# The input in a second, transposed layout, and its mean square through a product with ones

## The chip, the cores and the metric

The kernel runs on one core of a Trainium2 chip. The metric is the device time of one execution in microseconds; the profile and the trace are of one profiled execution. Engines: PE is TensorE (matmul), PEld its weight loads, DVE is VectorE, ACT is ScalarE, POOL is GpSimd, SP issues most of the DMAs. ACT issues DMAs too.

## The reference, cut to what matters

One layer of an encoder with 256 tokens and a width of 2048, all in float32. Only the first lines bear on the change:

```python
def rms_norm(x, w):
    y = x * lax.rsqrt(jnp.mean(x * x, axis=-1, keepdims=True) + EPS)
    return y * w

h = rms_norm(x, norm_mix_pre)
proj = jnp.einsum('bsd,dc->bsc', h, w_in)          # [256, 10240]
qa, ka, va, qn, kn, vn, gates = jnp.split(proj, split_at, axis=-1)
qa = apply_rope(qa, cos, sin); ka = apply_rope(ka, cos, sin)
...
x = x + rms_norm(y, norm_mix_post)
```

After it come two attentions (differential and neighbourhood), gates, an output projection with its norm and residual, and an MLP of width 8192 with squared ReLU. The factor rsqrt(mean(x²) + eps) is one number per token. It can be applied after the projection, and the kernel does so: it multiplies the rows of cos and sin by it (for qa and ka), or the values on their way out of PSUM.

## The kernel before, in words

Every float32 product is made of parts: a matrix w is split into hi (rounded to float32r by a cast on ACT) and lo = w - hi (a subtraction on DVE), both in `split` (L115 and L116). The activations are split likewise and lie as [128 | hi 256 | lo 256], so that one matmul with hi of the weight (L191, 512 wide) and one with lo (L192, 256 wide) make a product.

`wgroup` computes 512 columns of a projection, transposed, in four PSUM banks of [128 columns, 512]; it goes over the 2048 rows of the weight in four chunks of four row blocks. The pool `mm` holds exactly four such banks. A bank is emptied by `halves`: ACT copies its right half (L254), DVE adds that to the left half (L256). `agroup` is its counterpart for values (L229 to L231). `load` issues one weight chunk of 1 MB from SP into one of three buffers.

The first group is qa with columns QA to QA + 512. The lines around the change:

- The input x comes in four pieces of 512 columns, as [128 tokens, 2, 512], from SP (L144, L149), between the first three chunks of the weight (L146, L98).
- `x_parts(i)` transposes four blocks of x on TensorE (L268, against the identity) into a PSUM bank, and makes hi (L273, ACT, times the gain g_pre) and lo (L274, DVE) of them in hT.
- `x_squares(i)` squares a piece of x on ACT with a sum along the row (L345), so ssx holds sums per token, tokens on partitions.
- `prelude(ch)` is called ahead of chunk ch of the first group: it traces `x_parts` one chunk ahead, and the squares at chunks 2 and 3.
- `postlude` is called in the last chunk, after the products of bank 0 and ahead of its emptying: it issues small inputs, calls `row_scales` and `head_constants`.
- `row_scales` adds up ssx (L300), takes the mean plus eps (L85) to the power -0.5 on POOL (L88; rx is [128 tokens, 2]), and by `along_tokens` makes of it a row of all tokens on all partitions, rxb [128, 256]: a diagonal matrix on DVE (L77), a product with ones on TensorE (L78), a copy on ACT (L79). Then rxs (L303), and cosT and sinT times rxb (L304, L305).

The emptying of a qa or ka bank goes on with `rope_evac`: products with sinT and cosT, a sum, and the split in parts (L385 to L388, L371, L372).

The order of the instructions on each engine is made by a planner at build time, from the order in which they are traced and from its own estimates of their times; `tc.issue_after` adds an order by hand. At run time each engine takes its instructions in that order.

Of the kernel before, what the change touches and what calls it, by code (L numbers as in the profile page):

```python
# [17 lines left out]
P = 128  # L18
D = 2048
# [19 lines left out]
def encoder_layer(ctx: ExitStack, tc: tile.TileContext, a, out):  # L39
# [32 lines left out]
    def along_tokens(r, b, name):  # L72
        """r [P tokens, token tile] as a row of all tokens, on all partitions."""
        ps = bank(f"{name}_p")
        for t in range(2):
            dg = t1k(f"{name}_d{t}")
            nc.vector.tensor_scalar_mul(dg[:, :P], ident, r[:, t : t + 1])  # L77
            nc.tensor.matmul(ps[:, t * P : (t + 1) * P], ones, dg[:, :P], start=True, stop=True)  # L78
        nc.scalar.copy(b, ps[:, :T])  # L79

    def inv_rms(ss, n, name, r=None):
        """(ss / n + eps) ** -0.5, per partition."""
        w = ss.shape[1]
        ms_ = small(w, f"{name}_m")
        nc.vector.tensor_scalar(ms_, ss, 1.0 / n, EPS, op0=ALU.mult, op1=ALU.add)  # L85
        if r is None:
            r = small(w, f"{name}_r")
        nc.gpsimd.tensor_tensor(r, ms_, expo[:, :w], op=ALU.pow)  # L88
        return r

# [1 line left out]
    last_load = [None]  # L92

    def load(src, k0, nk, c0, cw, name):
        """Rows k0*128.. of a weight: [P, nk, cw]."""
        raw = wp.tile([P, nk, cw], F32, tag="raw", name=f"{name}_w")
        view = src[k0 * P : (k0 + nk) * P, c0 : c0 + cw].rearrange("(k p) c -> p k c", p=P)
        last_load[0] = nc.sync.dma_start(raw, view).ins  # L98
        return raw

    def split(raw, name, pieces=2, after=()):
        """Two float32r parts whose sum is raw. after[s] are instructions that go ahead of piece s."""
        _, nk, cw = raw.shape
        hi = wp.tile([P, nk, cw], F32R, tag="hi", name=f"{name}_h")
        lo = wp.tile([P, nk, cw], F32R, tag="lo", name=f"{name}_l")
        for s in range(pieces):
            part = (
                (slice(None), slice(s * nk // pieces, (s + 1) * nk // pieces))
                if nk > 1
                else (slice(None), slice(None), slice(s * cw // pieces, (s + 1) * cw // pieces))  # L110
            )
            with ExitStack() as order:
                for ins in after[s] if after else ():
                    order.enter_context(tc.issue_after(ins))
                nc.scalar.copy(hi[part], raw[part])  # L115
                nc.vector.tensor_sub(lo[part], raw[part], hi[part].bitcast(F32))  # L116
        return hi, lo
# [3 lines left out]

# [1 line left out]
    g_pre = const.tile([P, KD], F32, name="g_pre")  # L123
# [6 lines left out]
    nc.gpsimd.memset(ones, 1.0)  # L130
    x = a["x"]
    xv = x.rearrange("(t p) c -> p t c", p=P)
    xp = []
    first = []
    for i in range(4):
        xt = page([P, 2, 512], F32, f"x_{i}")
        xi = xv[:, :, i * 512 : (i + 1) * 512]
        xp.append(xt)
        if i == 0:
            raw = wp.tile([P, 4, 512], F32, tag="raw", name="first0_w")  # L140
            view = a["w_in"][: 4 * P, QA : QA + 512].rearrange("(k p) c -> p k c", p=P)
            for h in range(2):
                cs = slice(h * 256, (h + 1) * 256)
                nc.sync.dma_start(xt[:, :, cs], xi[:, :, cs])  # L144
                for k in range(h * 2, h * 2 + 2):
                    nc.sync.dma_start(raw[:, k], view[:, k])  # L146
            first.append(raw)
        else:
            nc.sync.dma_start(xt, xi)  # L149
            if i < 3:  # L150
                first.append(load(a["w_in"], i * 4, 4, QA, 512, f"first{i}"))
    g_mlp = const.tile([P, KD], F32, name="g_mlp")
# [19 lines left out]
    def advance(n):  # L172
        """Trace the next n stages of the attention heads that wait for their turn, and one chore."""
        if chores:
            with tc.issue_after(last_load[0]):
                chores.pop(0)()
        for _ in range(n):
            if pending:
                g = pending.pop(0)
                if next(g, None):  # L180
                    pending.append(g)

    def wgroup(src, c0, act, nk, evac, name, first=(), hook=None, mid=None, after={}, k_first=False, inner=None):
        """out^T of 512 columns: weights stationary. act(k) is [P, hi 256 | lo 256]."""
        ps = [bank(f"{name}_p{b}", True) for b in range(4)]
# [34 lines left out]
    def agroup(src, c0, stat, nk, evac, name, tail=1, between=None):  # L220
        """out of 512 columns: activations stationary. stat(k, t) is (hi, lo) of [P, 128].
        The last ``tail`` chunks go token tile by token tile; between(i) may trace instructions
        ahead of the i-th of the second tile's products there and returns the last of them."""
        ps = [bank(f"{name}_p{t}", True) for t in range(2)]
# [26 lines left out]
    def halves(ps, name):  # L251
        """The sum of the two halves of a bank, in SBUF."""
        r = t1k(f"{name}_r")
# [4 lines left out]

# [1 line left out]
    hT = [page([P, 2, 512], F32R, f"hT{i}") for i in range(8)]  # L260

    def x_parts(i):
        """The transpose of four tiles of x times the gain, in two parts [P, hi | lo]."""
        acts = []
        for k in range(i * 4, i * 4 + 4):
            pt = bank(f"hT_t{k}")
            for t in range(2):
                nc.tensor.transpose(  # L268
                    pt[:, t * P : (t + 1) * P], xp[i][:, t, (k % 4) * P : (k % 4 + 1) * P], ident
                )  # L270
            d = hT[k // 2][:, k % 2]
            g = g_pre[:, k : k + 1]
            acts.append(nc.scalar.activation(d[:, :T], pt[:, :T], AF.Copy, scale=g).ins)  # L273
            nc.vector.scalar_tensor_tensor(  # L274
                d[:, T:], pt[:, :T], g, d[:, :T].bitcast(F32), op0=ALU.mult, op1=ALU.subtract
            )

        return acts
# [16 lines left out]

    ssx = const.tile([P, 8], F32, name="ssx")

    def row_scales():
        sx = small(2, "sx")
        nc.vector.tensor_reduce(sx, ssx.rearrange("p (t h) -> p t h", h=4), axis=AX.X, op=ALU.add)  # L300
        inv_rms(sx, D, "rx", rx)
        along_tokens(rx, rxb, "rxb")
        nc.vector.tensor_scalar_mul(rxs, rx, SCALE)  # L303
# [15 lines left out]

    # Position bias: row (h, i) of rpbp holds the bias of row offset i - 3 at column offsets  # L320
    # -63..63. Each is written 64 times at a pitch of 127 and read at a pitch of 126.
    def skew_write(h):
# [18 lines left out]

    def x_squares(i):
        for t in range(2):
            j = junk512("jx0").rearrange("p a b -> p (a b)")
            nc.scalar.activation(  # L345
                j, xp[i][:, t], AF.Square, accum_out=ssx[:, t * 4 + i : t * 4 + i + 1]
            )

    def postlude():
# [15 lines left out]

# [1 line left out]
    oT = {}  # L367
# [6 lines left out]
    def product3(ps, stat, s_at, mov, m_at, start, stop):  # L374
        """ps (+)= stat^T @ mov, each given in two parts."""
        for i, (sp, mp) in enumerate(((0, 0), (0, 1), (1, 0))):
# [42 lines left out]
    def p_transposed(p, name):  # L419
        """[P queries, (t, keys)] -> [P keys, (key tile, queries)]"""  # L420
        pt = bank(f"{name}_pt")
# [171 lines left out]

# [1 line left out]
    mT = []  # L595
# [26 lines left out]

# [1 line left out]
    def mstat(k, t):  # L624
# [9 lines left out]
    for t in range(2):  # L634
        for h in range(2):
            nc.sync.dma_start(
                x2[t * 2 + h], x[t * P : (t + 1) * P, h * 1024 : (h + 1) * 1024]
            )
# [77 lines left out]

# [1 line left out]
    def first_up_inner(k):  # L718
# [103 lines left out]
def _host_arrays(inputs):  # L822
    f = {k: np.ascontiguousarray(v) for k, v in inputs.items()}
    arr = {
        "x": f["x"][0],
        "w_in": f["w_in"][0],
        "w_branch_a": f["w_branch_a"][0],
# [12 lines left out]
        "lam_k2": f["lam_k2"],  # L840
        # row offsets -3..3 are the ones that four rows reach
        "rpbp": np.pad(f["na_rpb"][0][:, 4:11], ((0, 0), (0, 0), (48, 48))),
# [30 lines left out]
```

## Time and profile before

| what | value |
|---|---|
| median of 3 runs | 1397.62 us (1397.48 to 1398.73) |
| span of the profiled execution | 1394.5 us |
| median of the runs less that span | 3.1 us |
| TensorE busy | 1374.6 us, 99% of the span |
| DVE, ACT, POOL busy | 835.8, 668.7, 7.9 us |
| first transpose, first product of qa | 3.95, 9.41 us |
| first product of ka | 36.58 us |

The profiled execution is known by its span, from the first to the last instruction. All times within it count from the span's start. A row of the trace in order of time reads: start, duration, engine, line, operation, written tile <- read tiles, shapes, count, and in brackets how long the engine had been idle and what ended that. Rows that follow each other on an engine are merged (x2, x4), their duration then being the stretch from the first start to the last end.

### The profile page before, as it was taken

The numbers are of one execution on the slowest core, as the hardware profiler recorded it, in microseconds if no ns is written. First come the engines' busy times: TensorE is split into PE (matmuls) and PEld (weight loads), VectorE is DVE, ScalarE is ACT, GpSimd is POOL, SyncE is SP. The second block draws the span as 40 slices with busy tenths as digits, with TensorE's granted clock in tenths as the row PEclk, the third lists the DMA queues.
The fourth block names the chain that finished last, engine by engine and source line by source line (L and its number), as shares of the span: only waits on it lengthen the run. The fifth ranks groups of instructions, "written<-read, shape, count | busy, mean of one in ns | idle before, by whom it ended". The sixth has DMA issues, their size and how long they took to land.

```text
span 1394.5 us, 17896 instructions
## 1 busy us (share of the span) xinstructions
PE 1374.6 (99%) x7240; PEld 1177.8 (84%) x7240; DVE 835.8 (60%) x1155; ACT 668.7 (48%) x1023; POOL 7.9 (1%) x19
## 2 busy tenths in 40 slices
PE   7999999999999999999899999999999999999997
PEld 6888888888888888888788888888888888888886
DVE  6868866676656565654755555555575554444445
ACT  7554554545444445543744444444464543334332
POOL 0000000000000000000000000000000000000000
PEclk9999999999999999999999999999999999999999
DMA  9674755564555555675455565656555556555551
GB/s 317 202 214 154 202 177 173 171 191 155 165 205 182 203 181 183 203 279 184 149 182 181 182 193 170 211 170 200 189 196 185 203 186 227 195 187 205 181 199 73
DMA packets 117490, 265.16 MB, mean 190 GB/s; under 512 B 15008, under 2 KB 16288, under 8 KB 109216
## 3 DMA queue, kind: packets, MB, share of 16 engines
q1 hardware_dynamic: 117264, 264.03, 57.3%
q8 instruction: 56, 0.92, 0.3%
q14 instruction: 26, 0.21, 0.0%
q10 hardware_dynamic: 144, 0.01, 0.0%
HBM read 261.92 MB, written 3.92 MB: 191 GB/s over the span
## 4 chain that ended last, share of the span: by engine, by line
PE 98%; DVE 1%; DMA 0%; ACT 0%; SPq 0%; issue 0%; DVEq 0%; POOLq 0%; POOL 0%; ACTq 0%
PE u_p L191 17%; PE u_p L192 9%; PE acc L779 8%; PE acc L778 8%; PE acc L777 8%; PE gb_p L191 4%; PE ga_p L191 4%; PE qa_p L191 2%; PE gb_p L192 2%; PE ga_p L192 2%; PE ka_p L191 2%; PE qn_p L191 2%; PE bb_p L191 2%; PE ba_p L191 2%; PE kn_p L191 2%; PE y_p L229 2%
## 5 line engine op out<-in xcount | busy, mean ns | idle before, releaser
L191 PE MATMUL u_p<-h2T,u_h 128*128 128x512 f32 x1024 | 359.9, 398 | 0.5 <-DVE r_m L85 0.5
L192 PE MATMUL u_p<-h2T,u_l 128*128 128x256 f32 x1024 | 284.3, 280 | 0.0
L116 DVE TENSOR_TENSOR d_l<-d_w,d_h 128x1024 fp32r<-128x1024 f32 x128 | 151.1, 1221 | 164.2 <-ACT d_h L115 163.7
L116 DVE TENSOR_TENSOR u_l<-u_w,u_h 128x1024 fp32r<-128x1024 f32 x128 | 151.1, 1222 | 146.0 <-ACT u_h L115 144.7
L191 PEld LDWEIGHTS u_p<-h2T,u_h 128*128 128x128 f32 x1024 | 192.0, 189 | 45.5 <-DVE r_m L85 0.9
L115 ACT CAST d_h<-d_w 128x1024 fp32r<-128x1024 f32 x128 | 128.3, 1052 | 191.1 <-PE acc L779 187.5
L778 PE MATMUL acc<-d_l,uh 128*128 128x512 f32 x512 | 199.0, 389 | 0.0
L779 PE MATMUL acc<-d_h,ul 128*128 128x512 f32 x512 | 198.9, 389 | 0.0
L777 PE MATMUL acc<-d_h,uh 128*128 128x512 f32 x512 | 198.2, 389 | 0.0
L192 PEld LDWEIGHTS u_p<-h2T,u_l 128*128 128x128 f32 x1024 | 193.8, 189 | 1.3
L115 ACT CAST u_h<-u_w 128x1024 fp32r<-128x1024 f32 x128 | 128.0, 1049 | 123.9 <-PE u_p L191 62.5
L778 PEld LDWEIGHTS acc<-d_l,uh 128*128 128x128 f32 x512 | 96.1, 188 | 20.1
L777 PEld LDWEIGHTS acc<-d_h,uh 128*128 128x128 f32 x512 | 96.1, 188 | 20.0
L779 PEld LDWEIGHTS acc<-d_h,ul 128*128 128x128 f32 x512 | 96.1, 188 | 19.8
L191 PE MATMUL gb_p<-hT,gb_h 128*128 128x512 f32 x256 | 90.4, 398 | 0.0
L191 PE MATMUL ga_p<-hT,ga_h 128*128 128x512 f32 x256 | 90.0, 397 | 0.0
L192 PE MATMUL gb_p<-hT,gb_l 128*128 128x256 f32 x256 | 71.4, 281 | 0.0
L192 PE MATMUL ga_p<-hT,ga_l 128*128 128x256 f32 x256 | 70.3, 280 | 0.0
L191 PEld LDWEIGHTS gb_p<-hT,gb_h 128*128 128x128 f32 x256 | 47.9, 188 | 11.5
L116 DVE TENSOR_TENSOR gb_l<-gb_w,gb_h 128x1024 fp32r<-128x1024 f32 x32 | 37.8, 1221 | 31.1 <-ACT gb_h L115 31.1
L191 PEld LDWEIGHTS ga_p<-hT,ga_h 128*128 128x128 f32 x256 | 47.4, 188 | 10.5
L116 DVE TENSOR_TENSOR y_l<-y_w,y_h 128x1024 fp32r<-128x1024 f32 x32 | 37.9, 1222 | 27.8 <-ACT y_h L115 27.8
(213 smaller groups left out, 2348.1 us busy)
## 6 DMA issues: line engine op xcount, KB each, us to landing
u_w<-in_w_up SPq DMA_DIRECT2D x64, 1024.0 KB, 5.4
d_w<-in_w_down SPq DMA_DIRECT2D x64, 1024.0 KB, 4.9
ga_w<-in_w_in SPq DMA_DIRECT2D x16, 1024.0 KB, 5.2
gb_w<-in_w_in SPq DMA_DIRECT2D x16, 1024.0 KB, 5.2
y_w<-in_w_out SPq DMA_DIRECT2D x16, 1024.0 KB, 5.1
ka_w<-in_w_in SPq DMA_DIRECT2D x8, 1024.0 KB, 6.1
va_w<-in_w_in SPq DMA_DIRECT2D x8, 1024.0 KB, 5.2
qn_w<-in_w_in SPq DMA_DIRECT2D x8, 1024.0 KB, 5.1
```

The costliest lines, as they stand in the source:

```text
L115: nc.scalar.copy(hi[part], raw[part])
L116: nc.vector.tensor_sub(lo[part], raw[part], hi[part].bitcast(F32))
L191: nc.tensor.matmul(ps[b], hi[:, k % 4, cs], mv, start=(k == 0), stop=False)
L192: nc.tensor.matmul(ps[b][:, :T], lo[:, k % 4, cs], mv[:, :T], start=False, stop=(k == nk - 1))
L229: nc.tensor.matmul(ps[t], sh, hi[:, k % 4], start=(k == 0), stop=False)
L777: nc.tensor.matmul(acc[t][c], uh[:, k % 4, ts_], hi[:, 0, cs], start=(k == 0), stop=False)
L778: nc.tensor.matmul(acc[t][c], uh[:, k % 4, ts_], lo[:, 0, cs], start=False, stop=False)
L779: nc.tensor.matmul(acc[t][c], ul[:, k % 4, ts_], hi[:, 0, cs], start=False, stop=(k == NK - 1))
```

## The change

The host gives x a second time, as xT of [128, 16, 256]: block k holds columns k*128 to k*128+127 of x on the partitions, and all tokens along the row. The kernel loads it in place of x at the start, into four tiles of [128, 4, 256]. The first tile comes from ACT's queue, in two pieces, behind g_pre; the first weight chunk goes out at once from SP in four pieces, then x^T and half chunks of the weight alternate. `x_parts` reads x^T from SBUF and needs no transposes and no PSUM. `x_squares` squares a tile on ACT and adds its four blocks on DVE into ssx, now [128, 256]. `row_scales` multiplies ones with ssx, which sums over the partitions and puts the result on all of them, and two narrow products give the sums with tokens on partitions; DVE takes the mean plus eps of both, and POOL the power -0.5 of [128, 256] (rxb) and of [128, 2] (rx). The residual at L636 still reads x.

```diff
-    x = a["x"]
-    xv = x.rearrange("(t p) c -> p t c", p=P)
-    for i in range(4):
-        xt = page([P, 2, 512], F32, f"x_{i}")
...
-            for h in range(2):
-                cs = slice(h * 256, (h + 1) * 256)
-                nc.sync.dma_start(xt[:, :, cs], xi[:, :, cs])
-                for k in range(h * 2, h * 2 + 2):
-                    nc.sync.dma_start(raw[:, k], view[:, k])
...
-            nc.sync.dma_start(xt, xi)
-            if i < 3:
-                first.append(load(a["w_in"], i * 4, 4, QA, 512, f"first{i}"))
+    xT = [page([P, 4, T], F32, f"xT{i}") for i in range(4)]
+    first = [wp.tile([P, 4, 512], F32, tag="raw", name=f"first{i}_w") for i in range(3)]
...
+    nc.scalar.dma_start(xT[0][:, 0:1], a["xT"][:, 0:1])
+    nc.scalar.dma_start(xT[0][:, 1:4], a["xT"][:, 1:4])
+    for k in range(4):
+        nc.sync.dma_start(first[0][:, k], fv[0][:, k])
+    for i in range(1, 3):
+        nc.sync.dma_start(xT[i], a["xT"][:, i * 4 : i * 4 + 4])
+        for h in range(2):
+            nc.sync.dma_start(first[i][:, h * 2 : h * 2 + 2], fv[i][:, h * 2 : h * 2 + 2])
+    nc.sync.dma_start(xT[3], a["xT"][:, 12:16])
...
     def x_parts(i):
         acts = []
         for k in range(i * 4, i * 4 + 4):
-            pt = bank(f"hT_t{k}")
-            for t in range(2):
-                nc.tensor.transpose(
-                    pt[:, t * P : (t + 1) * P], xp[i][:, t, (k % 4) * P : (k % 4 + 1) * P], ident
-                )
+            src = xT[i][:, k % 4]
             d = hT[k // 2][:, k % 2]
             g = g_pre[:, k : k + 1]
-            acts.append(nc.scalar.activation(d[:, :T], pt[:, :T], AF.Copy, scale=g).ins)
+            acts.append(nc.scalar.activation(d[:, :T], src, AF.Copy, scale=g).ins)
             nc.vector.scalar_tensor_tensor(
-                d[:, T:], pt[:, :T], g, d[:, :T].bitcast(F32), op0=ALU.mult, op1=ALU.subtract
+                d[:, T:], src, g, d[:, :T].bitcast(F32), op0=ALU.mult, op1=ALU.subtract
             )
...
-    ssx = const.tile([P, 8], F32, name="ssx")
+    ssx = const.tile([P, T], F32, name="ssx")
+
+    def x_squares(i):
+        sq = page([P, 4, T], F32, f"xsq{i}")
+        nc.scalar.activation(sq, xT[i], AF.Square)
+        nc.vector.tensor_add(sq[:, 0:2], sq[:, 0:2], sq[:, 2:4])
+        if i == 0:
+            nc.vector.tensor_add(ssx, sq[:, 0], sq[:, 1])
+        else:
+            nc.vector.tensor_add(sq[:, 0], sq[:, 0], sq[:, 1])
+            nc.vector.tensor_add(ssx, ssx, sq[:, 0])
 
     def row_scales():
-        sx = small(2, "sx")
-        nc.vector.tensor_reduce(sx, ssx.rearrange("p (t h) -> p t h", h=4), axis=AX.X, op=ALU.add)
-        inv_rms(sx, D, "rx", rx)
-        along_tokens(rx, rxb, "rxb")
+        ps = bank("rx_p")
+        nc.tensor.matmul(ps[:, :T], ones, ssx, start=True, stop=True)
+        for t in range(2):
+            nc.tensor.matmul(
+                ps[:, T + t : T + t + 1], ssx[:, t * P : (t + 1) * P], ones[:, :1], start=True, stop=True
+            )
+        m = t2k("rx_m").rearrange("p a b -> p (a b)")
+        nc.vector.tensor_scalar(
+            m[:, : T + 2], ps[:, : T + 2], 1.0 / D, EPS, op0=ALU.mult, op1=ALU.add
+        )
+        nc.gpsimd.tensor_tensor(rxb, m[:, :T], expo[:, :1].to_broadcast([P, T]), op=ALU.pow)
+        nc.gpsimd.tensor_tensor(rx, m[:, T : T + 2], expo[:, :2], op=ALU.pow)
         nc.vector.tensor_scalar_mul(rxs, rx, SCALE)
         nc.vector.tensor_mul(cosT, cosT, rxb)
         nc.vector.tensor_mul(sinT, sinT, rxb)
...
-    def x_squares(i):
-        for t in range(2):
-            j = junk512("jx0").rearrange("p a b -> p (a b)")
-            nc.scalar.activation(
-                j, xp[i][:, t], AF.Square, accum_out=ssx[:, t * 4 + i : t * 4 + i + 1]
-            )
...
         "x": f["x"][0],
+        "xT": f["x"][0].T.reshape(KD, P, T).transpose(1, 0, 2),
```

More of the change, by code (lines that the diff above doesn't have):

```diff
@@ L130, in encoder_layer @@
     nc.gpsimd.memset(ones, 1.0)
-    x = a["x"]
-    xv = x.rearrange("(t p) c -> p t c", p=P)
-    xp = []
-    first = []
-    for i in range(4):
-        xt = page([P, 2, 512], F32, f"x_{i}")
[L137 to L141, printed above, removed]
-            for h in range(2):
-                cs = slice(h * 256, (h + 1) * 256)
-                nc.sync.dma_start(xt[:, :, cs], xi[:, :, cs])
-                for k in range(h * 2, h * 2 + 2):
-                    nc.sync.dma_start(raw[:, k], view[:, k])
-            first.append(raw)
-        else:
-            nc.sync.dma_start(xt, xi)
-            if i < 3:
-                first.append(load(a["w_in"], i * 4, 4, QA, 512, f"first{i}"))
+    xT = [page([P, 4, T], F32, f"xT{i}") for i in range(4)]
+    first = [wp.tile([P, 4, 512], F32, tag="raw", name=f"first{i}_w") for i in range(3)]
+    fv = [
+        a["w_in"][i * 4 * P : (i + 1) * 4 * P, QA : QA + 512].rearrange("(k p) c -> p k c", p=P)
+        for i in range(3)
+    ]
+    nc.scalar.dma_start(xT[0][:, 0:1], a["xT"][:, 0:1])
[7 more added lines that the diff above has]
+    nc.sync.dma_start(xT[3], a["xT"][:, 12:16])
     g_mlp = const.tile([P, KD], F32, name="g_mlp")
@@ L636, in encoder_layer @@
             nc.sync.dma_start(
-                x2[t * 2 + h], x[t * P : (t + 1) * P, h * 1024 : (h + 1) * 1024]
+                x2[t * 2 + h], a["x"][t * P : (t + 1) * P, h * 1024 : (h + 1) * 1024]
             )
```

## The prediction

> **What bounds the kernel now.** I read the page's parts on busy time and on the chain first, then the first 60 us by windows and in order of time, then the rows of the instructions that the change removes, and last those of the one operation that it makes much wider, the power on POOL.
>
> ```profile
> span 1394.5 us, 17896 instructions
> PE 1374.6 (99%) x7240; PEld 1177.8 (84%) x7240; DVE 835.8 (60%) x1155; ACT 668.7 (48%) x1023; POOL 7.9 (1%) x19
> PE 98%; DVE 1%; DMA 0%; ACT 0%; SPq 0%; issue 0%; DVEq 0%; POOLq 0%; POOL 0%; ACTq 0%
> ```
>
> TensorE is busy for 99% of the span and is 98% of the chain that ended last, so only two things can move the time: when its stream begins and what stands in it, or a hole torn into it. All that the change touches lies ahead of 40 us:
>
> ```profile
> 8.00:10.00 2.00, 0.81 (x3) 0.50 (x2) 1.14 (x3) 2.00 (x7) 0.00 (x0) 1.00 1.04 379
> 20.00:25.00 5.00, 5.00 (x32) 4.43 (x31) 4.96 (x13) 4.48 (x10) 0.71 (x1) 1.00 1.05 319
> 25.00:30.00 5.00, 5.00 (x33) 4.45 (x32) 4.28 (x8) 3.30 (x6) 0.00 (x0) 1.00 0.98 360
> ```
>
> The columns are stretch, length, busy PE, PEld, DVE, ACT, POOL, granted clock, DMA share, GB/s. TensorE has no gap from 10 us on; DVE is 86 to 99% busy in 20 to 30 us, and DVE works in order.
>
> **The start.** Transposes wait for x, ACT's casts and squares stand between them and the copies into hT, and the first product starts at 9.41:
>
> ```profile
> 3.95 1.08 PE L268 MATMUL hT_t<-ident,x 128*128 128x128 f32 x4 [3.95 <-DMA x<-in_x]
> 5.08 0.62 ACT L115 CAST qa_h<-first_w 128x512 fp32r<-128x512 f32 x1 [2.61 <-DMA first_w<-in_w_in]
> 5.73 0.69 DVE L116 TENSOR_TENSOR qa_l<-first_w,qa_h 128x512 fp32r<-128x512 f32 x1 [5.73 <-ACT qa_h L115]
> 7.14 0.63 ACT L345 ACTIVATE jx<-x 128x512 f32<-128x512 f32 x1 [1.45 <-DMA x<-in_x]
> 8.38 1.54 ACT L273 ACTIVATE hT<-hT_t,g_pre 128x256 fp32r<-128x256 f32 x4
> 8.87 1.66 DVE L274 SCALAR_TENSOR_TENSOR hT<-hT_t,g_pre,hT 128x256 fp32r<-128x256 f32 x4 [2.45 <-ACT hT L273]
> 9.41 0.79 PE qa_p L191
> ```
>
> The first x lands at 3.95, the first weight rows at 5.08. After the change the first product needs 128 KB of x^T (second issue of ACT's queue) and the first 256 KB of weights, now first on SP. Both should be there at about 4 to 4.5. One copy into hT (0.47 on ACT), one cast (0.62) and one subtraction (0.69 on DVE) give a first product at 5.7 to 6.3; I take 6.0, a gain of 3.4 us. The ends are 0, if ACT again takes squares ahead, and 4.
>
> **The transposes.** 32 leave TensorE; 8 of them stand before 9.41 and count in the start. The other 24 stand in the stream:
>
> ```profile
> 20.37 0.28 PE L192 MATMUL qa_p<-hT,qa_l 128*128 128x256 f32 x1
> 20.49 0.38 PE L268 MATMUL hT_t<-ident,x 128*128 128x128 f32 x2
> 20.62 0.48 PE L191 MATMUL qa_p<-hT,qa_h 128*128 128x512 f32 x1
> 20.94 0.28 PE L192 MATMUL qa_p<-hT,qa_l 128*128 128x256 f32 x1
> 31.60 0.61 PE L78 MATMUL rxb_p<-rxb_d,ones 128*128 128x128 f32 x4
> 31.96 0.47 PE L191 MATMUL qa_p<-hT,qa_h 128*128 128x512 f32 x1
> ```
>
> From 20.49 to 20.94 pass 0.45 us with two transposes in them, against 0.23 without: 0.22 for two, 2.6 for 24, and about 2.9 because six ran while the stream still went at half pace. The old row of scales (four passes, 0.36 from 31.60 to 31.96) goes; its three float32 products, one 256 wide and two of one column, add by the same rows some 0.6. Net -2.9 - 0.36 + 0.6 = -2.6. Together with the start the stream is 6.0 us ahead.
>
> **The pace of a young stream** is the same price twice:
>
> ```profile
> 10.21 0.63 PE L191 MATMUL qa_p<-hT,qa_h 128*128 128x512 f32 x1
> 10.85 0.63 PE L191 MATMUL qa_p<-hT,qa_h 128*128 128x512 f32 x1
> 15.12 0.40 PE L191 MATMUL qa_p<-hT,qa_h 128*128 128x512 f32 x1
> 15.48 0.40 PE L191 MATMUL qa_p<-hT,qa_h 128*128 128x512 f32 x1
> ```
>
> A pair of products takes 0.64 us at 10 and 0.36 at 15, though the granted clock of the windows says 1.00 throughout. From 9.41 to about 14.4 that costs 5.0 x (1 - 0.36/0.64) = 2.2 us. I take it as equal before and after at the start, and as due once more after any long hole. TensorE: Matmul & The Clock Gate, Part 1, in the Trainium skill says that the clock is halved after about 3.4 us without work and released after as long of it; these rows agree on the factor.
>
> **The squares.** Eight squares of 128x512 on ACT (0.63 and a 0.19 read each, some 5 us) become four of 128x1024, about 1.05 each by the cast of that size below: ACT gets lighter. DVE gets four adds of 128x512 (0.69 above, 0.62 in a row) and seven of 128x256 (0.35 to 0.42): 5.0 us more where it is 86 to 99% busy. What covers them is that DVE also begins some 3.5 us earlier and no longer waits for transposes. Cover gone, the late parts of the weights would cost TensorE up to 5 us. I take 0, since the weights of the third chunk on have several us of lead, and keep 5 as the upper end.
>
> **The power on POOL.** Before, POOL raised 128x2 values and TensorE spread them along the tokens; now POOL raises 128x256, then 128x2. DVE's product for rxs and the two for cosT and sinT wait for it, and behind them on DVE, in program order, stand the additions (L256) that empty the four qa banks. There are four such banks, so ka can't start before.
>
> ```profile
> L88 POOL TENSOR_TENSOR dr_r<-dr_m,expo x4: 689/716/952, 113.1 to 193.5; 128x2 f32<-128x2 f32 x4
> L88 POOL TENSOR_TENSOR ry<-ry_m,expo x2: 547/550/552, 664.6 to 670.9; 128x1 f32<-128x1 f32 x2
> L88 POOL TENSOR_TENSOR rd_r<-rd_m,expo x2: 537/540/544, 1380.2 to 1387.5; 128x1 f32<-128x1 f32 x2
> L88 POOL TENSOR_TENSOR rx<-rx_m,expo x1: 711/711/711, 21.7 to 21.7; 128x2 f32<-128x2 f32 x1
> 665.13 1.42 DVE L657 SCALAR_TENSOR_TENSOR x<-yw,ry,x 128x512 f32<-128x512 f32 x2 [0.66 <-POOL ry L88]
> 0.87 0.10 POOL L128 MEMSET expo<- 128x4 f32 x1
> 0.91 0.20 POOL L130 MEMSET ones<- 128x128 f32 x1
> 19.69 0.63 ACT L345 ACTIVATE jx<-x 128x512 f32<-128x512 f32 x1
> 21.19 0.15 DVE L300 TENSOR_REDUCE sx<-ssx 128x2 f32<-128x8 f32 x1
> 34.05 0.42 DVE L304 TENSOR_TENSOR cosT<-cosT,rxb 128x256 f32<-128x256 f32 x1
> 34.38 0.42 DVE L305 TENSOR_TENSOR sinT<-sinT,rxb 128x256 f32<-128x256 f32 x1
> 35.30 0.42 DVE L256 TENSOR_TENSOR rope_s<-qa_p,rope_r 128x256 f32<-128x256 f32 x1 [0.50 <-ACT rope_r L254]
> 36.58 0.39 PE L191 MATMUL ka_p<-hT,ka_h 128*128 128x512 f32 x1
> L115 ACT CAST d_h<-d_w 128x1024 fp32r<-128x1024 f32 x128 | 128.3, 1052 | 191.1 <-PE acc L779 187.5
> 59.05 0.24 PE va_p L229
> ```
>
> One column takes 0.545 us, two take 0.711: 0.166 us for one more. DVE's start at 665.13, 0.58 after the power's at 664.55, shows that the time is real. Bounds for 256 columns: from below a plain POOL operation, (0.20 - 0.10) / 124 = 0.0008 us per column, so 0.75 us in all; from above 0.545 + 255 x 0.166 = 42.9 us (35.5 by the closest pair, 0.552 and 0.689). The same operation is nearer than a memset, so I take 42.9.
>
> When does it start? The sums stood at 21.19 before. Now DVE begins 3.5 earlier and has 5.0 more to do, which makes 22.7; the last quarter of x^T comes with as many bytes ahead of it as the last x had, whose squares ran at 19.69, and its square (1.05), three adds (1.4), the products and the scaling of the sums follow. I take 25 (22 to 28) for the power, hence 67.9 for rxb; then the small power (0.71), rxs, cosT, sinT and the first L256 (1.5) make 70.1 for the first free bank. The stream would have reached ka at 36.58 - 6.0 = 30.5: a hole of 39.6 us, and 2.2 for the pace after it. In words for any length X of the power: nothing while X is under about 3.5 us, then X - 3.5, and 2.2 more once the hole is a few us long.
>
> **The sum.** The span is 1394.5, and the median of the runs, 1397.6, lies 3.1 above, which the change doesn't touch. -3.4 - 2.6 + 39.6 + 2.2 = +35.8: a span of 1430.3 and a time of 1433.4.
>
> **Rivals.** First, on the other side: the power runs at the rate of a plain POOL operation, 0.75 us, and hides in the 3.5 us. Then the 6.0 us stand: 1391.6 (1389 to 1396, the upper end with the DVE adds uncovered and a start that moves less). For it: memset's row; two points make a poor line. Against it: the second column's 0.166 is some 200 times memset's. It decides from X below 3.5 us, and some gain is left to X = 8. GPSIMD Engine Reference, section 3.1, in the Trainium skill states about 2.6 cycles per element at 1.2 GHz for a two-input elementwise operation; by that 256 columns are an estimated 0.55 us above the start-up and the time would be this rival's. The page measured an addition; no run here shows that a power keeps it, and the 0.166 differs from it already.
>
> Second: the power's loop overlaps its columns once there are many. A third of the slope, 0.06, gives X = 15.8, a hole of 12.3 and 2.2: 1406 (1398 to 1414 for 0.035 to 0.08). Nothing in the trace shows it.
>
> Third: X is 42.9, but DVE's order puts the emptying of the qa banks ahead of the waiting products. Then ka runs (36.58 to 59.05, 22.5 us, now 30.5 to 53.0) and the hole opens at its end, since L256 needs buffers that the waiting qa sums hold: 69.6 - 53.0 = 16.6, and 2.2: 1410. For it: the order is planned and not the program's. Against it: before, L304 and L305 stand ahead of L256.
>
> **How the numbers follow.** The long power with the old order 0.52, the short power 0.27, the overlapped one 0.13, the other order 0.08. The time is the first's, 1433; its own range is 1420 to 1440 (X from 35.5, power from 22 to 28, 0 to 5 for the adds). The range has to reach to the short power: 1390 to 1438, with 0.05 left out at each end. About 0.2% (2.8 us) is what this kernel's times can tell from no change. Faster: 0.27 less 0.03 near zero, 0.24; same: that and 0.03 of the overlapped case, 0.06; slower: 0.52 + 0.08 + 0.10 = 0.70.
>
> **What would show it.** Right: a POOL row of L88's kind, 128x256, of some 43 us beginning near 25; DVE waiting for POOL nearly as long at the cosT product; ka's first product near 70 and a pace of 0.64 after it; first product near 6.0 and no hT_t rows. Wrong: that POOL row under 8 us. The start is wrong if the first qa product stays above 7, the adds if TensorE waits for qa_l before 25.

## The result, and the profile after

The changed kernel takes 1434.88 us (median of 4 runs, 1433.52 to 1436.66) against 1398.12 us: a ratio of 1.0269 (95% interval 1.0254 to 1.0283), 36.8 us slower. The profiled execution took 1433.52 us with a span of 1431.7, 37.2 more than the span before.

The page of the changed kernel: span, busy time of the engines, granted clock in 40 slices of 36 us, and the chain.

```profile
span 1431.7 us, 17839 instructions
PE 1371.9 (96%) x7210; PEld 1175.1 (82%) x7210; DVE 840.1 (59%) x1163; ACT 667.3 (47%) x1010; POOL 49.2 (3%) x20
PEclk9589999999999999999999999999999999999999
PE 93%; POOL 3%; DVE 1%; DMA 1%; ACT 1%; issue 0%; ACTq 0%; DVEq 0%; POOLq 0%; SPq 0%
```

POOL stood at 7.9 us and 0% of the chain; now it has 49.2 and 3% of the chain, in which TensorE fell from 98 to 93%. The clock digits 5 and 8 stand in the second and third slice: TensorE idled there. All of it happens at the passage from qa to ka, behind ka's first products. The trace of the changed kernel in order of time, rows of TensorE, DVE and POOL:

```profile
6.42 0.79 PE L186 MATMUL qa_p<-hT,qa_h 128*128 128x512 f32 x1 [6.42 <-DVE hT L265]
28.67 0.41 DVE L297 TENSOR_TENSOR ssx<-ssx,xsq 128x256 f32<-128x256 f32 x1
31.75 0.59 PE L301 MATMUL rx_p<-ssx,ones 128*128 128x256 f32 x2
32.77 0.42 DVE L251 TENSOR_TENSOR rope_s<-qa_p,rope_r 128x256 f32<-128x256 f32 x1
33.10 0.42 DVE L307 TENSOR_SCALAR rx_m<-rx_p 128x258 f32<-128x258 f32 x1
33.24 0.50 PE L186 MATMUL ka_p<-hT,ka_h 128*128 128x512 f32 x1 [0.56 <-DVE rope_s L251]
33.67 41.19 POOL L310 TENSOR_TENSOR rxb<-rx_m,expo 128x256 f32<-128x256 f32 x1 [32.23 <-DVE rx_m L307]
74.84 0.70 POOL L311 TENSOR_TENSOR rx<-rx_m,expo 128x2 f32<-128x2 f32 x1
74.89 0.42 DVE L313 TENSOR_TENSOR cosT<-cosT,rxb 128x256 f32<-128x256 f32 x1 [37.96 <-POOL rxb L310]
76.64 0.43 DVE L251 TENSOR_TENSOR rope_s<-qa_p,rope_r 128x256 f32<-128x256 f32 x1
77.21 0.77 PE L186 MATMUL ka_p<-hT,ka_h 128*128 128x512 f32 x1 [39.48 <-DVE rope_s L251]
77.99 0.63 PE L186 MATMUL ka_p<-hT,ka_h 128*128 128x512 f32 x1
78.63 0.63 PE L186 MATMUL ka_p<-hT,ka_h 128*128 128x512 f32 x1
81.17 0.40 PE L186 MATMUL ka_p<-hT,ka_h 128*128 128x512 f32 x1
81.52 0.40 PE L186 MATMUL ka_p<-hT,ka_h 128*128 128x512 f32 x1
```

(L297 is the last add of the squares; L186, L251, L301, L307, L310 and L313 of the new file are the old L191, L256, the new product with ones, the scaling of the sums, the wide power and the old L304.) The wide power takes 41.19 us. DVE, having emptied one of the four qa banks at 32.77, stands 37.96 us at the product for cosT; the next bank is emptied at 76.64; TensorE, which worked on ka in the one free bank until 37.7, waits 39.48 us for it. When it comes back, a pair of products takes 0.64 us until about 80.5. Here the clock column shows why; the stretches of the changed kernel by windows (columns as before, the granted clock third from the end):

```profile
40.00:60.00 20.00, 0.00 (x0) 0.00 (x0) 0.00 (x0) 0.00 (x0) 20.00 (x1) 0.57 0.07 26
60.00:76.00 16.00, 0.00 (x0) 0.00 (x0) 1.09 (x4) 0.00 (x0) 15.54 (x2) 0.50 0.00 0
78.00:80.00 2.00, 2.00 (x8) 1.71 (x8) 1.93 (x6) 0.76 (x2) 0.00 (x0) 0.50 0.00 0
80.00:82.00 2.00, 2.00 (x12) 1.72 (x12) 1.97 (x7) 0.41 (x1) 0.00 (x0) 0.92 0.00 0
```

The clock goes to 0.50 in the hole and stays there for some 3 us after the first product. So the bill of the hole, from ka's first product to va's: 96.93 - 33.24 = 63.7 us, against 58.89 - 36.58 = 22.3 before: 41.4 more, 39.5 of wait and a remainder of 1.9, which I put down to the slow pace (its five pairs, from 77.21 to 80.47, account for 1.5). Against it stand 3.3 us by which ka's first product came earlier (33.24 for 36.58), which gives +38.0 at va; the spans differ by 37.2.

### The profile page after: what moved, and what is told of

Same layout as the page of the kernel before. It is cut to its first block, busy times and chain, and to the rows that moved or that the text cites. A ratio compares the mean times of both kernels' runs of the same rounds, so it can differ in the third digit from the quotient of the medians.

```text
span 1431.7 us, 17839 instructions
## 1 busy us (share of the span) xinstructions
PE 1371.9 (96%) x7210; PEld 1175.1 (82%) x7210; DVE 840.1 (59%) x1163; ACT 667.3 (47%) x1010; POOL 49.2 (3%) x20
## 4 chain that ended last, share of the span: by engine, by line
PE 93%; POOL 3%; DVE 1%; DMA 1%; ACT 1%; issue 0%; ACTq 0%; DVEq 0%; POOLq 0%; SPq 0%
PE u_p L186 17%; PE u_p L187 8%; PE acc L779 8%; PE acc L780 8%; PE acc L781 8%; PE gb_p L186 4%; PE ga_p L186 4%; POOL rxb L310 3%; PE gb_p L187 2%; PE ga_p L187 2%; PE qn_p L186 2%; PE bb_p L186 2%; PE kn_p L186 2%; PE ba_p L186 2%; PE y_p L224 2%; PE y_p L226 2%
## 5 line engine op out<-in xcount | busy, mean ns | idle before, releaser
L186 PE MATMUL u_p<-h2T,u_h 128*128 128x512 f32 x1024 | 359.1, 397 | 1.0 <-DVE h2T L676 1.0
L186 PEld LDWEIGHTS u_p<-h2T,u_h 128*128 128x128 f32 x1024 | 191.7, 188 | 45.6 <-DVE h2T L676 1.2
L186 PE MATMUL gb_p<-hT,gb_h 128*128 128x512 f32 x256 | 90.4, 398 | 0.0
L186 PE MATMUL ga_p<-hT,ga_h 128*128 128x512 f32 x256 | 90.0, 398 | 0.0
L186 PE MATMUL ka_p<-hT,ka_h 128*128 128x512 f32 x128 | 46.7, 409 | 40.0 <-DVE rope_s L251 40.0
L186 PEld LDWEIGHTS ka_p<-hT,ka_h 128*128 128x128 f32 x128 | 24.5, 193 | 45.9 <-issue 39.8
L186 PEld LDWEIGHTS gb_p<-hT,gb_h 128*128 128x128 f32 x256 | 47.9, 188 | 11.5
L186 PEld LDWEIGHTS ga_p<-hT,ga_h 128*128 128x128 f32 x256 | 47.5, 188 | 10.5
```

The source lines that it names most:

```text
L186: nc.tensor.matmul(ps[b], hi[:, k % 4, cs], mv, start=(k == 0), stop=False)
```

## The experiments

My theory was that the wide power and DVE's wait for it are the whole loss, and that the rest of the change gains. Its rivals: that POOL's operation disturbs others while it runs, that its length is a start-up, and that the new layout costs something itself. Ratios are to the kernel before, on the same chip, with 95% intervals; not all rows were measured on the same chip, so rows are compared by their ratios where it is close. The last column is from the one profiled execution of each. The powers of 128 and 16 columns leave the other columns without a power, and the kernel without adds leaves out sums, so these three don't compute the reference.

| kernel | us (median) | ratio | ka's first product |
|---|---|---|---|
| narrow power | 1399.57 | 1.0015 (1.0006 to 1.0024) | 38.3 |
| narrow, one queue | 1398.57 | 1.0010 (1.0001 to 1.0019) | 36.6 |
| narrow, adds left out | 1394.81 | 0.9984 (0.9975 to 0.9993) | 33.8 |
| before, x from ACT's queue | 1398.65 | 1.0010 (1.0001 to 1.0019) | 39.5 |
| power of 128 columns | 1415.99 | 1.0129 (1.0113 to 1.0145) | 35.3 |
| power of 16 columns | 1396.10 | 0.9992 (0.9982 to 1.0001) | 34.2 |
| before, idle wide power | 1397.59 | 1.0000 (0.9991 to 1.0009) | 38.0 |
| all qa banks emptied first | 1425.19 | 1.0199 (1.0184 to 1.0213) | 33.6 |
| adds on POOL | 1402.99 | 1.0042 (1.0030 to 1.0055) | 41.6 |
| adds on POOL, early products | 1403.32 | 1.0045 (1.0031 to 1.0059) | 41.4 |
| scales behind ka's first chunk | 1401.35 | 1.0030 (1.0020 to 1.0041) | 33.5 |
| that, early products | 1401.97 | 1.0032 (1.0020 to 1.0045) | 34.3 |

**The length of the power: 128 and 16 columns** (N in the edit).

```diff
-        nc.gpsimd.tensor_tensor(rxb, m[:, :T], expo[:, :1].to_broadcast([P, T]), op=ALU.pow)
+        nc.gpsimd.tensor_tensor(rxb[:, :N], m[:, :N], expo[:, :1].to_broadcast([P, N]), op=ALU.pow)
+        nc.vector.tensor_copy(rxb[:, N:], m[:, N:T])
```

Expected for 128:

> The changed kernel with the wide power over 128 of the 256 columns; the rest of rxb is copied on DVE without a power, so half the tokens get a wrong scale. My theory (length by the column): the POOL row takes 0.55 + 127 x 0.16 = 20.9 us, the hole shrinks by 20.3, time 1413 to 1416. Rival (a long start-up, as for code that has to be fetched, and few ns per column): the POOL row stays near 40 and the time near 1434.

and for 16:

> As the last, with 16 columns in the power. My theory: the POOL row takes 0.55 + 15 x 0.16 = 2.95 us and hides but for a part: a hole of at most 2 us ahead of or inside ka, time 1392 to 1396. Rival of the fixed start-up: 1434.

The POOL rows in order of time, first of the kernel with 128 columns:

```profile
36.11 20.97 POOL L310 TENSOR_TENSOR rxb<-rx_m,expo 128x128 f32<-128x128 f32 x1 [34.66 <-DVE rx_m L307]
```

and of the one with 16:

```profile
34.68 3.10 POOL L310 TENSOR_TENSOR rxb<-rx_m,expo 128x16 f32<-128x16 f32 x1 [33.23 <-DVE rx_m L307]
```

20.97 and 3.10, where 20.9 and 2.95 were expected: 0.158 us per column from 128 to 256 and 0.160 from 16 to 128. The line from one to two columns held over two powers of ten; a start-up that makes up most of the 41 us is excluded. With 16 columns TensorE waits 1.6 us in all for ka's banks, and the time, 1396.1, lies 0.1 above the expected 1392 to 1396.

**The power without the wait.** In the kernel before, a power of 128x256 on constants that nothing reads:

```diff
         inv_rms(sx, D, "rx", rx)
+        idle = page([P, 4, T], F32, "idle").rearrange("p a b -> p (a b)")
+        nc.gpsimd.tensor_tensor(
+            idle[:, :T], ones[:, :1].to_broadcast([P, T]), expo[:, :1].to_broadcast([P, T]), op=ALU.pow
+        )
```

> The kernel before with a power of 128x256 on POOL that nothing waits for, on constants. My theory (it is the wait, not the operation): a POOL row of about 41 us and a time within 1 us of the kernel before. Rival (a long POOL operation slows DVE at their common memory ports): DVE's 128x256 rows get longer than 0.42 beside it and the time rises by over 2 us.

POOL in order of time, and DVE's subtractions beside it (minimum, median, maximum in ns, first and last start):

```profile
23.08 41.14 POOL L303 TENSOR_TENSOR idle<-ones,expo 128x256 f32<-128x256 f32 x1
L116 DVE TENSOR_TENSOR ka_l<-ka_w,ka_h x8: 1215/1220/1226, 29.3 to 51.8; 128x1024 fp32r<-128x1024 f32 x8
```

The operation runs as long and costs nothing (1.0000), and DVE's 1220 ns are those of the kernel before (1219). It is the wait.

**Which wait: all four banks emptied first.** The products of cosT and sinT and the whole rotation are traced behind the four emptyings:

```diff
-        nc.vector.tensor_mul(cosT, cosT, rxb)
-        nc.vector.tensor_mul(sinT, sinT, rxb)
...
+        def evac(b, ps):
+            held.append(halves(ps, "rope"))
+            if b < 3:
+                return
+            nc.vector.tensor_mul(cosT, cosT, rxb)
+            nc.vector.tensor_mul(sinT, sinT, rxb)
+            for i, s in enumerate(held):
...
```

> The changed kernel; the products of cosT and sinT with rxb, and all of qa's rotation, are traced behind the emptying (L249, L251) of all four qa banks. My theory (TensorE waits for the banks, and DVE's order keeps them): ka runs in full from about 33 to 55, the hole moves behind it and ends with the power at about 75, so it shrinks from 39.5 to 18 to 20: time 1412 to 1416. Rival (TensorE would wait for rxb itself, or buffers of the emptied banks run out at once): a hole of over 35 and a time over 1430.

The DVE rows in order of time, and the longest wait of TensorE (total, times, longest):

```profile
78.19 0.43 DVE L400 TENSOR_TENSOR cosT<-cosT,rxb 128x256 f32<-128x256 f32 x1 [18.70 <-POOL rxb L310]
85.40 0.42 DVE L251 TENSOR_TENSOR rope_s<-ka_p,rope_r 128x256 f32<-128x256 f32 x1
PE va_p L224 <- DVE rope_s L251: 29.8, 1, 29.8
```

ka ran in full and the hole moved behind it, as the theory of the banks has it: TensorE doesn't need rxb, it needs DVE to get past it. But it was 29.8 us long and not 18 to 20. After the power DVE first does 7.2 us of qa's rotation before it empties a bank of ka, which I hadn't counted, and the power itself took 43.46 us here and not 41.19 (why stays open: the idle power in the experiment above ran beside a busy DVE in 41.14).

**The rest of the change without the wide power.** The power of [128, 2] is spread along the tokens as before; x^T, the queues and the squares stay:

```diff
-        nc.tensor.matmul(ps[:, :T], ones, ssx, start=True, stop=True)
...
-        nc.gpsimd.tensor_tensor(rxb, m[:, :T], expo[:, :1].to_broadcast([P, T]), op=ALU.pow)
+        inv_rms(ps[:, :2], D, "rx", rx)
+        along_tokens(rx, rxb, "rxb")
```

> The changed kernel, but the power is taken of [128, 2] alone and spread along the tokens as before; x^T, the two queues and the squares stay. My theory (the whole loss is the 41.19 us power that DVE waits for): no hole in TensorE, first qa product at 6.4, ka's first product at 32.5 to 33.5 in place of 36.58, and the changed kernel's 1434.9 less the hole of 39.5, the 0.6 ahead of ka and some 2 us of slow pace: 1391.5 to 1394.5. Rival (the new layout and its squares cost time by themselves): 1398 or more. Rival (a shorter hole stays, since DVE is full): 1395 to 1400 with a wait of ka_p or qa_p for DVE.

It took 1399.57: the wide power accounts for 35.3 us, and the rest of the change doesn't gain. Here my theory fell; the second rival named the right kind of wait. TensorE's waits in the first 130 us, and DVE in order of time, with one product of ka behind the restart:

```profile
PE qa_p L186 <- DVE hT L265: 7.6, 2, 6.0
PE rxb_p L78 <- DVE rxb_d L77: 3.8, 1, 3.8
PE ka_p L186 <- DVE rope_s L251: 0.7, 1, 0.7
31.22 0.43 DVE L297 TENSOR_TENSOR ssx<-ssx,xsq 128x256 f32<-128x256 f32 x1
31.56 2.37 DVE L116 TENSOR_TENSOR ka_l<-ka_w,ka_h 128x1024 fp32r<-128x1024 f32 x2
33.83 0.17 DVE L85 TENSOR_SCALAR rx_m<-rx_p 128x2 f32<-128x2 f32 x1
34.91 1.23 DVE L116 TENSOR_TENSOR ka_l<-ka_w,ka_h 128x1024 fp32r<-128x1024 f32 x1 [0.58 <-ACT ka_h L115]
36.05 0.48 DVE L77 TENSOR_SCALAR rxb_d<-ident,rx 128x128 f32<-128x128 f32 x2
39.06 0.63 PE L186 MATMUL ka_p<-hT,ka_h 128*128 128x512 f32 x1
```

The last add into ssx is done at 31.6, where the sums stood at 21.3 before; between the two narrow steps that follow, DVE works off subtractions of ka. TensorE, in order, stands still for 3.8 us at the product that spreads the scales, and restarts at the slow pace (39.06: 0.63 for a product, with the granted clock at 0.51 from 36 to 42 us).

**Is it the adds?** All but one of them left out of that kernel (so the scales are wrong):

```diff
-        nc.vector.tensor_add(sq[:, 0:2], sq[:, 0:2], sq[:, 2:4])
         if i == 0:
             nc.vector.tensor_add(ssx, sq[:, 0], sq[:, 1])
-        else:
-            nc.vector.tensor_add(sq[:, 0], sq[:, 0], sq[:, 1])
-            nc.vector.tensor_add(ssx, ssx, sq[:, 0])
```

> The kernel with the narrow power; the sums over the blocks of x^T are left out on DVE (all but one add of 128x256), so the mean square is wrong and only the time counts. My theory (the 5 us of adds are covered): within 0.5 us of the kernel with the narrow power. Rival (DVE is the bound of the first 30 us): up to 5 us less than it.

1394.81, 4.8 us less, with intervals that don't touch: the rival, almost to its full 5 us. TensorE's waits in the first 130 us, and TensorE in order of time:

```profile
PE qa_p L186 <- DVE hT L265: 7.3, 2, 6.4
PE ka_p L186 <- DVE rope_s L251: 0.8, 1, 0.8
10.25 2.07 PE L186 MATMUL qa_p<-hT,qa_h 128*128 128x512 f32 x4 [0.93 <-DVE hT L265]
33.82 0.48 PE L186 MATMUL ka_p<-hT,ka_h 128*128 128x512 f32 x1
```

The wait for the row of scales is gone, and ka starts at 33.82. Even so the gain over the kernel before is 2.8 us at ka and 0.16% in time, not the 6.0 that I had summed. The 4.8 us are the adds' price in this narrow form, not in every one: the kernel with 16 columns keeps all the adds, has no product that spreads the scales for TensorE to stand at, and took 1396.10, 3.5 us less than the narrow one, with intervals that don't touch either.

**The two queues.** First the narrow kernel with everything from SP (x^T block 0, weight rows 0, then the rest):

```diff
-    nc.scalar.dma_start(xT[0][:, 0:1], a["xT"][:, 0:1])
-    nc.scalar.dma_start(xT[0][:, 1:4], a["xT"][:, 1:4])
-    for k in range(4):
-        nc.sync.dma_start(first[0][:, k], fv[0][:, k])
+    nc.sync.dma_start(xT[0][:, 0:1], a["xT"][:, 0:1])
+    nc.sync.dma_start(first[0][:, 0], fv[0][:, 0])
+    nc.sync.dma_start(xT[0][:, 1:4], a["xT"][:, 1:4])
...
```

> The kernel with the narrow power, and all of x^T and the weights issued from SP (x^T block 0, weight rows 0, the rest of x^T's first tile, the other weight rows). If the second queue matters: the first qa product comes 0.5 us or more after 6.4 and the time rises by as much. If not (what lands decides, not who issues): within 0.5 us of the kernel with the narrow power.

Then the kernel before with its two first pieces of x from ACT's queue (`nc.scalar.dma_start` at L144):

> The kernel before, with the two first pieces of x issued from ACT's queue and the weights from SP: one part of the change alone. If the start was late because of the issue order: first qa product well before 9.41 and a gain of 1 to 3 us. If it was late because of what ACT does between (squares ahead of the copies into hT): first product at 9 to 9.5 and the time within 0.5 us of 1398.1.

The second queue brings nothing in either place. With one queue the first product comes at 5.84, not later, and the stream runs on without the wait that the two-queue kernel has for the rest of the first tile (0.93 and 1.68 us in two runs); the times, 1398.57 and 1399.57, are 1.0 us apart where 0.5 was expected, and their ratios lie within each other's intervals. In the kernel before, the second queue makes x later, which neither theory had: the first transpose waits until 5.77 and not 3.95, and ka starts at 39.5. In order of time, of that kernel:

```profile
5.77 1.08 PE L268 MATMUL hT_t<-ident,x 128*128 128x128 f32 x4 [5.77 <-DMA x<-in_x]
```

Four weight pieces of SP are on their way beside x, and they come earlier instead: the first weight cast starts at 3.51 and not 5.08. That x is late because they share the transfers fits this, but isn't shown by itself; x was also issued 0.4 us later, behind g_pre.

**The adds elsewhere.** In the kernel with one queue, the adds on POOL (`nc.gpsimd` in place of `nc.vector` in `x_squares`), and with it ten products of ones ahead of the stream:

```diff
+    wps = bank("warm_p")
+    for _ in range(10):
+        nc.tensor.matmul(wps[:, :P], ones, ones, start=True, stop=True)
     xT = [page([P, 4, T], F32, f"xT{i}") for i in range(4)]
```

> The kernel with the narrow power and one issuing queue, and the sums of squares added up on POOL, which is idle there, in place of DVE. My theory now (the 5 us of adds on DVE push the sums and what follows them behind the stream; TensorE waits 3.7 us for the row of scales and comes back at the slow pace, which costs some 2 us again): no wait of rxb_p or ka_p, ka's first product at 32 to 34 in place of 36.6, time 1392 to 1395. Rival (POOL is too slow for the adds, or its memory port slows DVE): the same wait or a longer one, time 1397 or more.

> The last kernel, with ten products of ones with ones on TensorE ahead of the stream, their result unused: they fill the time in which the kernel before transposed. Theory (removing the transposes also removed the work that ends the slow pace, so the slow stretch after the first product got longer or stays as long though it starts earlier): the slow pace of 0.64 us per pair ends within 3 us of the first product, and the time falls by 1 to 2 us. Rival (the slow stretch has nothing to do with earlier work): within 0.5 us of the last kernel.

The first theory fell: 1402.99, the rival's side. TensorE's longest later wait, the POOL row of two wide adds, and DVE's subtractions beside them in 20 to 36 us (minimum, median, maximum):

```profile
PE rx_p L303 <- POOL ssx L298: 5.3, 1, 5.3
20.62 2.55 POOL L293 TENSOR_TENSOR xsq<-xsq 128x512 f32<-128x512 f32 x2 [19.17 <-ACT xsq L292]
L116 DVE TENSOR_TENSOR qa_l<-qa_w,qa_h x2: 1750/1904/2059, 24.3 to 26.3; 128x1024 fp32r<-128x1024 f32 x2
```

The adds end at 36.7 on POOL, and DVE's two subtractions in these rows take 1.75 and 2.06 us beside them, in place of 1.22. The early products did what they were to do at the start. TensorE in order of time with them:

```profile
1.17 4.63 PE L134 MATMUL warm_p<-ones 128*128 128x128 f32 x20 [1.17 <-POOL ones L130]
6.25 0.50 PE L190 MATMUL qa_p<-hT,qa_h 128*128 128x512 f32 x1 [0.45 <-DVE hT L269]
6.70 0.40 PE L190 MATMUL qa_p<-hT,qa_h 128*128 128x512 f32 x1
```

The full pace of 0.35 us per pair holds from the second product on, but the time doesn't fall: the stream runs into the first weights, and ka's start is set by the sums on POOL (41.4 and 41.6).

**The scales later.** In the kernel with one queue, `row_scales` and qa's rotation are traced in ka's second chunk, behind the emptying of qa's four banks:

```diff
-        row_scales()
         head_constants()
...
+    def scale_and_rope(ch):
+        if ch != 1:
+            return
+        row_scales()
+        for dst, b, s in held:
...
```

> The kernel with the narrow power and one issuing queue, adds on DVE; the row of scales and the rotation of qa are traced in ka's second chunk, behind the emptying of qa's four banks and ka's first chunk. Theory (the sums come too late for a place right behind qa, and TensorE, in order, stands still at the product that spreads the scales): no wait of over 1 us in TensorE from 12 to 60 us, ka's first product at 32 to 33.5, and 3.5 to 6 us less than the kernel with one queue: 1392 to 1395. Rival (DVE's 5 us of adds reach TensorE at another place, as a wait for ka_l or for ka's banks): 1396 or more.

and with the early products again:

> The last kernel with ten products of ones with ones ahead of the stream, their result unused. Theory (the slow pace after the first product is the price of an idle TensorE before it, and with no later hole the gain reaches the end): 1 to 2 us less than the last kernel, 1390.5 to 1394. Rival (the stream then waits for the first weights instead): within 0.5 us of the last kernel, with waits of qa_p for qa_h.

The rival once more: 1401.35. ka starts at 33.5 without a wait for the scales (1.7 us for its first bank remain, where under 1 was expected), but the rotations of qa and ka now meet on DVE, and TensorE's wait moves to va:

```profile
PE va_p L225 <- DVE rope_s L252: 4.0, 1, 4.0
```

With the early products the wait for va stays at 4.0 us, and another for weights appears; 1401.97, 0.6 above the last kernel and so nearer the rival. No variant that computes the reference beat the kernel before.

## Why the prediction was right, step by step

**The power (right).** 42.9 us from four rows of one and two columns, 41.19 measured. The second rival, an overlap of many columns, isn't there: 0.158 us per column at 128 to 256. By GPSIMD Engine Reference, section 3.1, in the Trainium skill, about 2.6 cycles per element, the wide power would have been an estimated 0.55 us above its start-up; the measurement decides, and that figure (for an addition, there) doesn't hold for a power.

**The hole (right in its cause; right in length by luck, as misses cancel).** DVE stood for POOL at the cosT product, and TensorE for the banks behind it, as forecast. 39.6 predicted, 39.5 measured. The power began at 33.67 and not at 25, which lengthens the hole by 8.7. But TensorE went on until 37.7 and not to 30.5, which takes 7.2 away: its stream reached ka later, at 33.24, and DVE had emptied one bank ahead of the cosT product, which let ka's first products run. The power itself was 1.7 shorter. Two of the signs that I had named therefore didn't come: the power's start near 25, and ka's first product near 70. The order was a piece of my third rival.

**The slow pace behind the hole (right).** 2.2 predicted; 1.5 by the rows of the restart, 1.9 as the remainder. The trace agrees with TensorE: Matmul & The Clock Gate, Part 1, in the Trainium skill: half the clock in the hole (0.50), back some 3 us into the work.

**The 5 us of adds at nothing (wrong).** The term that failed. The adds cost 4.8 us in the narrow kernel. I looked for them at the weights of the third chunk; they came up at the sums themselves, behind which I had placed the power at 25. In the changed kernel the last add ends at 29.1 (28.67 and 0.41). Then 2.7 us pass until the product with ones, which has its place in TensorE's order at 31.75 (TensorE doesn't idle ahead of it), and 1.9 more until the power at 33.67. So the adds are a part of the late start and the order of the engines another. In the narrow kernel without adds the power still began at 28.54, 3.5 later than I had it; how the 8.7 divide in the changed kernel isn't measured.

**The 6.0 us of the head start (half).** 3.0 of the 3.4 at the first product (6.42). At ka 2.8 are left of 6.0 even without the adds, in that experiment by 33.82 against 36.58. The step behind it that failed is the pace taken as equal before and after. Before, TensorE reached full pace 3.6 us after the first product (the row below, of four products, has it); I had read 5.0.

```profile
13.06 1.19 PE L191 MATMUL qa_p<-hT,qa_h 128*128 128x512 f32 x4
```

The granted clock is of no help there, as the trace's record of it begins only with the full pace (at 12.85 us before, at 12.07 in the changed kernel), and the windows ahead of that print 1.00 for want of one. By these starts the slow stretch lasted 2.8 to 10.5 us from the first product in the nine kernels without transposes and without early products, and 3.4 to 5.5 in the three with transposes. It differs so much from one execution to the next that its length isn't shown to come from the change; ten products ahead of the stream removed it. In the run without adds it ended at about 14, nearly 3 us more at slow pace than before, worth 1.3 us; the wait for x^T at 10.25 is 0.9 and the later start 0.4. That makes 2.6 of the missing 3.2; the rest isn't settled.

**The sum.** +35.8 predicted, +36.8 measured (1433.4 against 1434.88). The hole's cause and the power's price were right. That the sum came so close is in part luck: the hole's misses cancel, and of the 2.7 us by which the head start at ka was taken too large (6.0 for 3.3), 0.8 come back between va and the end of the span (38.0 against 37.2), which isn't explained. The first rival, a short power, would not have given 1391.6 either: with 16 columns, 3.10 us, the time was 1396.1.

## What to carry to other kernels

Before you widen an operation, look for two rows of it that differ in size and draw the line through them: a narrow operation that costs nothing can have a price per column that makes the wide one long (41.19 us on POOL, where one of DVE's additions of 128x256 takes 0.42). Then ask not who reads the result but who stands behind the reader: here TensorE needed four banks that had nothing to do with the power, and lost 39 us because their emptying stood behind it on an engine that works in order. And work that moves from one busy engine to another isn't covered merely because it starts earlier; find the first of its results that the engine which bounds the time waits for, and date that.

## What the runs showed of the hardware that I had not expected

POOL's float32 power takes about 0.16 us per column of 128 partitions, nearly the same from 1 to 256 columns, and leaves DVE alone (1220 ns beside it). POOL's adds don't: beside them DVE's 128x1024 subtraction took 1.75 and 2.06 us in place of 1.22. And TensorE's stream began at half pace, for 2.8 to 10.5 us (waits for data included), though the granted clock of those windows reads 1.00; ten products of constants ahead of it removed that in both kernels that had them. Whether transposes ahead of the stream shorten it, these runs don't show.
